# Sums of squares of keys and queries from three bfloat16 parts, on one Trainium2 core

## The chip, the core and the metric

The kernel runs on 1 core of one Trainium2 chip. Its time is the device time in microseconds (us) of one execution. Five engines take part. TensorE multiplies matrices (PE in the rows, its weight loads PEld). VectorE (DVE) and ScalarE (ACT) do elementwise work, GpSimd (POOL) a little of it, and SyncE (SP) issues most DMAs. Every engine takes its instructions in order; between engines, semaphores hold an instruction until the data it needs is there.

## What is computed

The reference is one block of a network: a pooling mixer and sparse attention, then an expert layer and a gate. The change touches only the normalization of queries and keys, for 256 tokens, 16 query heads and 4 key groups of 64 channels each:

```python
def rmsnorm(x, w):
    xf = x.astype(jnp.float32)
    y = xf * lax.rsqrt(jnp.mean(xf * xf, axis=-1, keepdims=True) + RMS_EPS)
    return (y * w.astype(jnp.float32)).astype(x.dtype)

u, q, kc, vc, ksl, vsl, kwn, vwn, gl = jnp.split(hn @ w_in[i], offsets, axis=-1)
q = rmsnorm(q.reshape(B, S, H, dk), q_norm_w[i])
k_slc = rmsnorm(ksl.reshape(B, S, G, dk), k_norm_w[i])
k_win = rmsnorm(kwn.reshape(B, S, G, dk), k_norm_w[i])
```

The mean goes over the 64 channels of one head, so for each token and head a sum of 64 squares is needed.

## The kernel before

All data is float32. A matrix of weights comes in loads of 512 KB (`load`, tile `wraw`, three buffers, issued by SP as soon as VectorE has finished with the buffer's last user). Each load is split into a high part (ScalarE, tile `whi`, L139) and the rest (VectorE, tile `wlo`, L140), and three products of the parts stand for one float32 product. `gemm` makes one tile of 128 output channels by 256 tokens in 16 steps of three products, and needs two loads; I call the first and the second load's steps the halves of a tile.

The projections run in this order: four tiles of keys and values for compression, then four tiles of keys (`head_tiles(0)`, output tile `att`), then the values (`pval`), then eight tiles of queries (`head_tiles(1)` and `head_tiles(2)`, output `qk`), then the pooling input. I number the key tiles 1 to 4 and the query tiles 1 to 8. After each of the twelve tiles, VectorE merges the result out of the accumulator (`merge`, L205), ScalarE squares it (`qsq`, L501), and a generator, `sumsq`, is put into a list of side work. The list is advanced from inside the steps of the following tile, so that TensorE's instructions for the sums come in the middle or at the end of the next tile. There `sumsq` takes the 128 channels by 256 tokens of squares as stationary weights, in two blocks of 128 tokens, against `sel2`, a matrix of 128 by 2 that picks the two heads of the tile:

```python
p = pg([128, 2, 2], "pn")
for tb in range(2):
    mm(p[:, tb], sq[:, tb * 128:tb * 128 + 128], sel2)
```

These are plain float32 products; the trace shows two passes of the array for each, four for a tile. `norm` then makes the factors of all heads when four tiles are through.

TensorE's order is the order in which the program is written (`manual_schedule` on PE). On ScalarE and VectorE a scheduler orders the instructions by its own estimates, after the prologue. In the stretch of the key tiles these two also work on the inputs of the compression: sums of the two accumulators and their scaling (`kt`, L415 to L417) and shifted copies (`kcf`, L420, ScalarE).

Of the kernel before, what the change touches and what calls it, by code (L numbers as in the profile page):

```python
# [9 lines left out]
BF = mybir.dt.bfloat16  # L10
# [3 lines left out]
OP = mybir.AluOpType  # L14
# [4 lines left out]
D, S, NH, NG, DK, NC, NE = 2048, 256, 16, 4, 64, 15, 128  # L19
# [35 lines left out]
def body(tc, I, out, dump=None):  # L55
# [4 lines left out]
    V, G, A, T = nc.vector, nc.gpsimd, nc.scalar, nc.tensor  # L60
# [9 lines left out]
    def a2(shape, name, dt=F32):  # L70
        return pools["w"].tile(shape, dt, name=name, tag="a2", bufs=7)

    def a1(shape, name, dt=F32):
        return pools["w"].tile(shape, dt, name=name, tag="a1", bufs=6)
# [4 lines left out]
    def a0(shape, name, dt=F32):  # L79
        return pools["w"].tile(shape, dt, name=name, tag="a0", bufs=12)  # L80

    def pm(shape, name="pmm"):
        return ps.tile(shape, F32, name=name, tag="mm", bufs=2)

    def pv(shape, name="pvv"):
        return ps.tile(shape, F32, name=name, tag="v", bufs=4)

    def pg(shape, name="pgg"):
        return ps.tile(shape, F32, name=name, tag="g", bufs=2)

    def mm(o, l, r, start=True, stop=True, skip=False):
        T.matmul(o, l, r, start=start, stop=stop, skip_group_check=skip)  # L92
# [22 lines left out]
    def cbv(n):  # L115
        o, w = CB[n]
        return cb[:, o:o + w]
# [32 lines left out]
    def later(g, first=False):  # L150
        gens.insert(0 if first else len(gens), [g, 0])
# [46 lines left out]
    def gemm(p, src, x, rate=0, units=None, before=None, wide=True):  # L198
        for half in range(2):
            u = units and units[half] or unit(src[:, half * 1024:(half + 1) * 1024])  # L200
            gemm_k(p, u, x, range(half * 8, half * 8 + 8), rate, before, wide)

    def merge(dst, p, rb, wide=True):
        if not wide:
            return V.tensor_tensor(dst, p[:, 0], rb, op=OP.mult)  # L205
        A.copy(dst, p[:, 1])
        V.tensor_tensor(dst, p[:, 0], dst, op=OP.add)
        return V.tensor_tensor(dst, dst, rb, op=OP.mult)
# [105 lines left out]
    def sq1(k0):  # L314
        for k in (k0, k0 + 2):
            x = xT[:, k:k + 2].rearrange("p k t -> p (k t)")
            if k == 0:
                rs["sq"] = kcf[:, 2048:2560]
                A.activation(rs["sq"], x, AF.Square)
                continue  # L320
            t = a2([128, 512], "sqb")
            A.activation(t, x, AF.Square)
            V.tensor_tensor(rs["sq"], rs["sq"], t, op=OP.add)
            if k == 14:
                V.tensor_tensor(s1.acc, rs["sq"][:, 0:256], rs["sq"][:, 256:512], op=OP.add)
# [115 lines left out]
    G.memset(kcz, 0.0)  # L441
    G.memset(vcz, 0.0)
    nc.scalar.dma_start(c1, I["cw2"])
    sel2 = cbv("sel2")
    selb = a2([128, 4, 128], "selb", F32R)
    A.copy(selb, cbv("selb").rearrange("p (c m) -> p c m", c=4))
    qw8 = a0([128, 1], "qw8")
# [1 line left out]
    def sumsq(c, sq, ms):  # L449
        yield 3  # L450
        p = pg([128, 2, 2], "pn")
        for tb in range(2):
            mm(p[:, tb], sq[:, tb * 128:tb * 128 + 128], sel2)
        V.tensor_copy(ms[:, :, 2 * c:2 * c + 2], p)
        yield

    def norm(b, ms):
        yield 2
        m2 = ms.rearrange("p t h -> p (t h)")
        V.tensor_copy(m2, rsqrt_v(m2, 16, "nr"))  # L460
        rk = a1([128, S], "rk", F32R)
        G.memset(rk.bitcast(F32), 0.0)
        yield 8
        p = pg([8, S], "pnt")
        for tb in range(2):
            T.transpose(p[:, tb * 128:tb * 128 + 128], ms[:, tb], ident)
        A.copy(rk[0:8], p)
        V.tensor_tensor(rk[32:40], p, rk.bitcast(F32)[0:8], op=OP.subtract)
        yield 4
        for c in range(4):  # L470
            p = pv([128, S], "pselb")
            mm(p, selb[:, c], rk)
            if b == 0:
                br, gp = divmod(c, 2)
                for gi in range(2):
                    h = slice(gi * 64, gi * 64 + 64)
                    V.scalar_tensor_tensor(kz[h, gp, br, gi], kraw[h, c], smv("kw")[h], p[h], op0=OP.mult, op1=OP.mult)
            else:
                q = qT[:, 4 * (b - 1) + c]
                V.scalar_tensor_tensor(q, q, qw8, p, op0=OP.mult, op1=OP.mult)  # L480
            yield
        ready.add("n%d" % b)

    def head_tiles(b, rate, ahead=None):
        ms = a0([128, 2, 8], "ms")
        for c in range(4):
            p = pm([128, 2, S])
            if b + c:
                gemm(p, I["wt"][4 * b + c], hx, rate, wide=False)
            else:  # L490
                gemm(p, I["wt"][0], hx, rate, (rs["u"], None), {1: lambda: sq1(8), 4: lambda: sq1(12), 9: rs_front}, False)
                rs["b"] = s1.rstd_back(rs["p"])
                ready.add("rstd")
            dst = kraw[:, c] if b == 0 else qT[:, 4 * (b - 1) + c]
            i = merge(dst, p, rs["b"], False)
            if b == 0 and c == 3:
                state["main"]["keys"] = i.ins
            if ahead:
                ahead(c)
            sq = a1([128, S], "qsq")  # L500
            A.activation(sq, dst, AF.Square)  # L501
            later(sumsq(c, sq, ms), True)

        def finish():
            yield 4
            yield from norm(b, ms)
        later(finish(), True)

    head_tiles(0, 0.3, load_w1)


# [71 lines left out]
    for tb in range(2):  # L583
        p = pv([128, 128], "prn")
        T.transpose(p, rs["b"][:, tb * 128:tb * 128 + 128], ident)
        V.tensor_copy(rn[:, tb:tb + 1], p[:, 0:1])
    for s, (w, kn, kl) in enumerate(((304, 3, 3), (256, 4, 4))):
        acc = [(pm, pv)[s]([128, w], "pval") for _ in range(2)]
        k0 = 0
        while k0 < KC:  # L590
# [4 lines left out]
            for k in range(n // w):  # L595
                kc = k0 + k
                a, b = hi[:, k * w:(k + 1) * w], lo[:, k * w:(k + 1) * w]
# [34 lines left out]
    def attention(gp, qb):  # L632
# [124 lines left out]
        V.tensor_tensor(t[d + (1, q)], pt, t.bitcast(F32)[d + (0, q)], op=OP.subtract)  # L757

    head_tiles(1, 0.6)
    cx = Pair("cx")  # L760
    later(attention(0, 0))
    later(attention(0, 1))
    head_tiles(2, RATE)
    later(attention(1, 0))
    later(attention(1, 1))
# [29 lines left out]
    for g in (3, 2, 1, 0):  # L795
# [4 lines left out]
        for cc in range(2):  # L800
            p = pm([128, 2, S])
# [9 lines left out]
    for m in range(KC):  # L811
        p = pm([128, 2, S])
# [302 lines left out]
    for j in range(4):  # L1115
        u = pu[0] if j == 0 else unit(I["pj"][j])
        for i in range(4):
            p = pv([128, S], "pproj")
# [26 lines left out]
    for m in range(KC):  # L1145
        gs[m] = pv([128, 2, S], "pgate")
        sq = {2 * i + 1: (lambda k=8 + 4 * m + i: s3.add(x2[:, k], pools["p"], V)) for i in range(4)} if m < 2 else None
# [113 lines left out]
```

## Time and profile before

| quantity | value |
|---|---|
| median of 3 runs | 2021.57 us (2021.44 to 2022.99) |
| the profiled execution | 2023.23 us, its span in the trace 2021.5 us |
| TensorE busy | 2011.7 us |
| VectorE, ScalarE busy | 1505.6 us, 995.6 us |
| granted TensorE clock | 1.00 of full speed, mean over the span |
| products for the sums of squares | 48 passes between 44.7 and 166.6 us |

The profile is of one execution. A timeline row gives the start of a run of equal instructions, the time from the first start to the last end, engine, source line, operation, written and read tiles, form and count; brackets at its end give the engine's idle time just before and what ended it. Neighbouring instructions of an engine overlap in such rows (the last end is modelled for TensorE), so the pace is read from start to start.

### The profile page before, as it was taken

To read this page: it belongs to the slowest core of one execution; us is meant where nothing else is said; L and a number is where in the kernel's file an instruction comes from. 1 tells how busy PE (TensorE), PEld (TensorE's weight loads), DVE (VectorE), ACT (ScalarE), POOL (GpSimd) and SP (SyncE) were. 2 spreads that over 40 slices of the span, in tenths; PEclk is the share of its full clock that TensorE was granted. 3 is DMA by queue.
4 is the path that set the end of the run, shared out by engine and by line. 5 is a ranking of instruction groups with operands and counts; after the bars stand their busy time and mean duration, and the time that the engine had idled before them with its cause. 6 is when DMAs were issued, how large, how long until landed. Compare 5 with 4: busy or idle time off the path is not lost.

```text
span 2021.5 us, 31175 instructions
## 1 busy us (share of the span) xinstructions
PE 2011.7 (100%) x11922; PEld 1733.8 (86%) x11922; DVE 1505.6 (74%) x2532; ACT 995.6 (49%) x1471; POOL 91.5 (5%) x112
## 2 busy tenths in 40 slices
PE   9999999999999999999999999999999999999999
PEld 7999988888888888888888888888888888888888
DVE  7657767767888897677777778888887555666686
ACT  6445544545444544444444454445445444455554
POOL 3100023000000000000000000000000000001000
PEclk9999999999999999999999999999999999999999
DMA  8843246655555556555555556556555666666665
GB/s 293 224 130 103 95 127 208 223 175 181 185 188 186 181 186 190 179 184 173 186 183 173 186 169 197 177 188 211 196 177 187 197 194 192 193 192 191 192 195 158
DMA packets 104469, 371.32 MB, mean 184 GB/s; under 512 B 12377, under 2 KB 14953, under 8 KB 104041
## 3 DMA queue, kind: packets, MB, share of 16 engines
q1 hardware_dynamic: 100656, 358.06, 55.6%
q10 hardware_dynamic: 1728, 6.47, 0.9%
q0 software_dynamic: 1936, 4.79, 0.9%
q8 instruction: 94, 1.54, 0.3%
q14 instruction: 55, 0.45, 0.1%
HBM read 365.05 MB, written 4.78 MB: 183 GB/s over the span
## 4 chain that ended last, share of the span: by engine, by line
PE 95%; DMA 3%; DVE 1%; ACT 1%; issue 0%; SPq 0%; ACTq 0%; DVEq 0%
PE pmm L92 45%; PE pV L92 33%; PE pgate L92 4%; PE pq L92 4%; PE pG L92 2%; DMA wraw<-in_wt_dram 1%; PE pl L92 1%; PE po L92 1%; PE pval L92 1%; PE pc L92 1%; DVE wlo L140 1%; DMA wraw<-in_w_dram 1%; PE pt L711 1%; PE pproj L92 1%; ACT whi L139 0%; DMA wraw<-in_wv_dram 0%
## 5 line engine op out<-in xcount | busy, mean ns | idle before, releaser
L140 DVE TENSOR_TENSOR wlo<-wraw,whi 128x1024 fp32r<-128x1024 f32 (+2 forms) x675 | 820.4, 1224 | 311.7 <-ACT whi L139 309.1
L139 ACT ACTIVATE whi<-wraw 128x1024 fp32r<-128x1024 f32 (+2 forms) x675 | 708.6, 1050 | 577.9 <-PE pV L92 171.7
L92 PE MATMUL pmm<-xn,whi 128*128 128x512 f32 x2048 | 716.3, 397 | 0.0
L92 PE MATMUL pV<-whi,ahl 128*128 128x512 f32 x2032 | 636.3, 391 | 0.0
L92 PE MATMUL pmm<-xn,wlo 128*128 128x256 f32 x2048 | 552.4, 280 | 0.0
L92 PEld LDWEIGHTS pV<-whi,ahl 128*128 128x128 f32 x2032 | 381.6, 188 | 78.8
L92 PEld LDWEIGHTS pmm<-xn,whi 128*128 128x128 f32 x2048 | 378.0, 188 | 79.9
L92 PE MATMUL pV<-wlo,ahl 128*128 128x512 f32 x1016 | 395.8, 390 | 0.5 <-DVE wlo L140 0.5
L92 PEld LDWEIGHTS pmm<-xn,wlo 128*128 128x128 f32 x2048 | 386.4, 189 | 9.5
L92 PEld LDWEIGHTS pV<-wlo,ahl 128*128 128x128 f32 x1016 | 190.9, 188 | 39.3 <-DVE wlo L140 1.0
L964 ACT COPY A<-pmm 128x256 f32<-128x256 f32 x112 | 41.8, 373 | 179.4 <-PE pmm L92 179.3
L1038 ACT ACTIVATE ahl<-A 128x512 fp32r<-128x512 f32 x111 | 69.8, 631 | 119.8 <-PE pV L92 118.5
L92 PE MATMUL pmm<-hn,whi 128*128 128x256 f32 x640 | 120.8, 283 | 0.0
L92 PE MATMUL pmm<-hn,wlo 128*128 128x256 f32 x320 | 106.9, 340 | 0.9 <-DVE wlo L140 0.8
L92 PEld LDWEIGHTS pmm<-hn,whi 128*128 128x128 f32 x640 | 98.5, 190 | 4.9 <-issue 3.8
L1039 DVE TENSOR_TENSOR ahl<-A,ahl 128x512 fp32r<-128x512 f32 x111 | 76.3, 690 | 34.7 <-ACT ahl L1038 33.3
L92 PE MATMUL pq<-x,whi 128*128 128x512 f32 x256 | 92.0, 400 | 0.0
L92 PE MATMUL pgate<-x,whi 128*128 128x512 f32 (+1 forms) x272 | 89.7, 385 | 0.0
L92 PE MATMUL pmm<-cx,whi 128*128 128x512 f32 x256 | 89.3, 398 | 0.0
L965 DVE TENSOR_TENSOR A<-pmm,A 128x256 f32<-128x256 f32 x112 | 47.3, 422 | 52.5 <-ACT A L964 52.2
L987 DVE TENSOR_TENSOR e<-e,gT 128x1024 f16<-128x1024 f16 x64 | 78.0, 1219 | 0.0
L981 DVE TENSOR_TENSOR oh<-idT,iob 128x1024 f16<-128x1024 bf16 x64 | 77.8, 1216 | 0.0
(284 smaller groups left out, 1907.1 us busy)
## 6 DMA issues: line engine op xcount, KB each, us to landing
wraw<-in_ut_dram SPq DMA_DIRECT2D x256, 512.0 KB, 4.2
wraw<-in_v_dram SPq DMA_DIRECT2D x256, 512.0 KB, 4.5
wraw<-in_wt_dram SPq DMA_DIRECT2D x40, 512.0 KB, 3.6
wraw<-in_wo_dram SPq DMA_DIRECT2D x32, 512.0 KB, 3.7
wraw<-in_wq_dram SPq DMA_DIRECT2D x32, 512.0 KB, 3.6
wraw<-in_wg_dram SPq DMA_DIRECT2D x32, 512.0 KB, 4.6
wraw<-in_w_dram SPq DMA_DIRECT2D x8, 512.0 KB, 4.8
wraw<-in_wv_dram SPq DMA_DIRECT2D x5, 456.0 KB, 8.4
```

The lines of the kernel that those rows point to most:

```text
L92: T.matmul(o, l, r, start=start, stop=stop, skip_group_check=skip)
L139: A.activation(hi[:, q], raw[:, q], AF.Copy)
L140: i = V.tensor_tensor(lo[:, q], raw[:, q], hi.bitcast(F32)[:, q], op=OP.subtract)
L711: T.transpose(pt[:, i, kb], e[:, i, kb * 128:kb * 128 + 128], ident)
L964: A.copy(a, p[:, 1])
L965: evac = V.tensor_tensor(a, p[:, 0], a, op=OP.add)
L981: V.tensor_tensor(oh2, idT[:, 1, t0:t0 + TB].unsqueeze(2).to_broadcast([128, TB, 128]), iob.unsqueeze(1).to_broadcast([128, TB, 128]), op= ...
L987: V.tensor_tensor(e2, e1.unsqueeze(1).to_broadcast([128, 2, TB, W]), gT[:, :, t0:t0 + TB].unsqueeze(3).to_broadcast([128, 2, TB, W]), op=O ...
L1038: A.activation(pair[:, :, 0], a, AF.Copy)
L1039: V.tensor_tensor(pair[:, :, 1], a, pair[:, :, 0].bitcast(F32), op=OP.subtract)
```

## The change

The squares are cut into three bfloat16 parts: the rounded square, the rounded rest, and what is left of that. Each part is a stationary operand of its own, `sel2` is converted to bfloat16 once, and the three products of a token block are summed in the accumulator. For a tile this puts six 16-bit products in the place of two float32 products (four passes), two conversions more on ScalarE and two subtractions more on VectorE.

```diff
-    sel2 = cbv("sel2")
+    sel2 = a0([128, 2], "sel2", BF)
+    V.tensor_copy(sel2, cbv("sel2"))
...
         for tb in range(2):
-            mm(p[:, tb], sq[:, tb * 128:tb * 128 + 128], sel2)
+            for a in range(3):
+                mm(p[:, tb], sq[:, a, tb * 128:tb * 128 + 128], sel2, start=a == 0, stop=a == 2)
...
             sq = a1([128, S], "qsq")
             A.activation(sq, dst, AF.Square)
-            later(sumsq(c, sq, ms), True)
+            sp = a2([128, 3, S], "qsp", BF)
+            A.copy(sp[:, 0], sq)
+            V.tensor_tensor(sq, sq, sp[:, 0], op=OP.subtract)
+            A.copy(sp[:, 1], sq)
+            V.tensor_tensor(sp[:, 2], sq, sp[:, 1], op=OP.subtract)
+            later(sumsq(c, sp, ms), True)
```

The four new lines are one chain: conversion (ScalarE, L505), subtraction (VectorE, L506), conversion (ScalarE, L507), subtraction (VectorE, L508). TensorE's order is the old one but for the products of the sums; in the place of each tile's four passes stand six weight loads with six products. On the other two engines the scheduler placed the chain as follows.

ScalarE at the third key tile, before (`qsq` is the tile's square; the three splits `whi` are for the values' weights):

```order
L501 ACTIVATE qsq<-att 128x256
L139 ACTIVATE whi<-wraw 128x912 x3
L501 ACTIVATE qsq<-att 128x256
```

And now:

```order
L503 ACTIVATE qsq<-att 128x256
L139 ACTIVATE whi<-wraw 128x912
L505 CAST qsp<-qsq 128x256
L139 ACTIVATE whi<-wraw 128x912
L507 CAST qsp<-qsq 128x256
L139 ACTIVATE whi<-wraw 128x912
L503 ACTIVATE qsq<-att 128x256
```

The two conversions stand between the splits of three loads of the values' weights, and the second conversion is behind the second of these splits.

VectorE at the same place, before (from the split of the third key tile's weights to the merge of the fourth, `att`):

```order
L140 TENSOR_TENSOR wlo<-wraw,whi 128x1024
L205 TENSOR_TENSOR att<-pmm,rs_456 128x256
L140 TENSOR_TENSOR wlo<-wraw,whi 128x912 x2
L205 TENSOR_TENSOR att<-pmm,rs_456 128x256
L454 COPY ms<-pn 128x2x2
```

And now:

```order
L140 TENSOR_TENSOR wlo<-wraw,whi 128x1024
L140 TENSOR_TENSOR wlo<-wraw,whi 128x912
L506 TENSOR_TENSOR qsq<-qsq,qsp 128x256
L140 TENSOR_TENSOR wlo<-wraw,whi 128x912
L508 TENSOR_TENSOR qsp<-qsq,qsp 128x256
L205 TENSOR_TENSOR att<-pmm,rs_458 128x256
```

The second subtraction, which writes the third part, is behind the split of the second load of the values' weights.

VectorE at the third and fourth query tiles, before (a merge, `qk`, and the split of weights right behind it):

```order
L205 TENSOR_TENSOR qk<-pmm,rs_456 128x256
L140 TENSOR_TENSOR wlo<-wraw,whi 128x1024
L454 COPY ms<-pn 128x2x2
L140 TENSOR_TENSOR wlo<-wraw,whi 128x1024
L205 TENSOR_TENSOR qk<-pmm,rs_456 128x256
```

And now:

```order
L205 TENSOR_TENSOR qk<-pmm,rs_458 128x256
L140 TENSOR_TENSOR wlo<-wraw,whi 128x1024
L506 TENSOR_TENSOR qsq<-qsq,qsp 128x256
L508 TENSOR_TENSOR qsp<-qsq,qsp 128x256
L456 COPY ms<-pn 128x2x2
```

The subtractions stand behind the split that follows the merge, and ahead of the copy of the sums (`ms`).

ScalarE at these tiles, before:

```order
L139 ACTIVATE whi<-wraw 128x1024 x2
L501 ACTIVATE qsq<-qk 128x256
L139 ACTIVATE whi<-wraw 128x1024 x2
L501 ACTIVATE qsq<-qk 128x256
L139 ACTIVATE whi<-wraw 128x1024 x2
```

And now:

```order
L139 ACTIVATE whi<-wraw 128x1024 x2
L503 ACTIVATE qsq<-qk 128x256
L505 CAST qsp<-qsq 128x256
L507 CAST qsp<-qsq 128x256
L139 ACTIVATE whi<-wraw 128x1024 x2
L503 ACTIVATE qsq<-qk 128x256
L505 CAST qsp<-qsq 128x256
L507 CAST qsp<-qsq 128x256
```

The conversions stand directly behind the square and ahead of the next splits.

## Rows read from the trace of the kernel before

**Rows 1.** The page, busy time of each engine, share of the span, instructions

```profile
PE 2011.7 (100%) x11922; PEld 1733.8 (86%) x11922; DVE 1505.6 (74%) x2532; ACT 995.6 (49%) x1471; POOL 91.5 (5%) x112
```

**Rows 2.** Timeline of TensorE: start us, us, engine, line, op, out<-in, form, count, [idle]

```profile
130.61 0.50 PE L92 MATMUL pn<-cb,qsq 128*128 128x2 f32 x4
130.98 0.36 PE L92 MATMUL pmm<-hn,wlo 128*128 128x256 f32 x1
```

**Rows 3.** The same, at a group of 16-bit products

```profile
828.47 0.40 PE L92 MATMUL pmm<-xn,whi 128*128 128x512 f32 x1
828.71 0.64 PE L92 MATMUL pG<-e,oh 128*128 128x64 f16 x16
829.19 0.36 PE L92 MATMUL pmm<-xn,wlo 128*128 128x256 f32 x1
```

**Rows 4.** Timeline of VectorE, query tiles: merges, one split

```profile
108.27 0.42 DVE L205 TENSOR_TENSOR qk<-pmm,rs 128x256 f32<-128x256 f32 x1 [1.57 <-PE pmm L92]
...
122.45 0.42 DVE L205 TENSOR_TENSOR qk<-pmm,rs 128x256 f32<-128x256 f32 x1 [0.62 <-PE pmm L92]
...
128.65 0.42 DVE L205 TENSOR_TENSOR qk<-pmm,rs 128x256 f32<-128x256 f32 x1 [0.51 <-PE pmm L92]
129.79 1.23 DVE L140 TENSOR_TENSOR wlo<-wraw,whi 128x1024 fp32r<-128x1024 f32 x1 [0.71 <-ACT whi L139]
...
134.97 0.42 DVE L205 TENSOR_TENSOR qk<-pmm,rs 128x256 f32<-128x256 f32 x1
...
163.11 0.42 DVE L205 TENSOR_TENSOR qk<-pmm,rs 128x256 f32<-128x256 f32 x1
```

**Rows 5.** Timeline of TensorE, the sums of squares of those query tiles

```profile
110.95 0.50 PE L92 MATMUL pn<-cb,qsq 128*128 128x2 f32 x4
...
124.77 0.50 PE L92 MATMUL pn<-cb,qsq 128*128 128x2 f32 x4
...
136.81 0.50 PE L92 MATMUL pn<-cb,qsq 128*128 128x2 f32 x4
...
166.38 0.50 PE L92 MATMUL pn<-cb,qsq 128*128 128x2 f32 x4
```

**Rows 6.** Timeline of TensorE, the key tiles

```profile
44.71 0.61 PE L92 MATMUL pn<-cb,qsq 128*128 128x2 f32 x4 [0.27 <-ACT qsq L501]
45.17 0.36 PE L92 MATMUL pmm<-hn,wlo 128*128 128x256 f32 x1
...
51.82 0.61 PE L92 MATMUL pn<-cb,qsq 128*128 128x2 f32 x4 [0.65 <-ACT qsq L501]
...
58.48 0.51 PE L92 MATMUL pn<-cb,qsq 128*128 128x2 f32 x4
...
60.35 0.41 PE L92 MATMUL pval<-whi,hn 128*128 128x304 f32 x1 [0.66 <-DVE att L205]
...
64.57 0.61 PE L92 MATMUL pn<-cb,qsq 128*128 128x2 f32 x4 [0.20 <-ACT qsq L501]
```

**Rows 7.** Timeline of ScalarE, the key tiles

```profile
43.13 1.06 ACT L139 ACTIVATE whi<-wraw 128x1024 fp32r<-128x1024 f32 x1 [2.65 <-DMA wraw<-in_wt_dram]
44.24 0.42 ACT L501 ACTIVATE qsq<-att 128x256 f32<-128x256 f32 x1
44.56 0.63 ACT L415 COPY kt<-pkv 128x256 f32<-128x256 f32 x2
...
48.03 3.30 ACT L420 COPY kcf<-kt 64x256 f32<-64x256 f32 x8
```

**Rows 8.** Timeline of VectorE, before and in the first key tiles

```profile
29.28 0.69 DVE L323 TENSOR_TENSOR kcf<-kcf,sqb 128x512 f32<-128x512 f32 x1 [1.05 <-ACT sqb L322]
...
45.36 0.75 DVE L416 TENSOR_TENSOR kt<-pkv,kt 128x256 f32<-128x256 f32 x2
```

**Rows 9.** Loads of weights issued between 44 and 62 us: time to landing

```profile
DMA to landing us min/median/max: 5.7/8.4/10.3
```

**Rows 10.** Timeline of TensorE, the warm-up products

```profile
1.23 5.91 PE L92 MATMUL idle_p<-idle_w 128*128 128x512 bf16 x18 [1.23 <-DVE idle_w L304]
```


## The prediction

> **What bounds the kernel now.** I read the page first: TensorE is busy for 2011.7 of the span's 2021.5 us, VectorE and ScalarE for three quarters and for half [rows 1]. So a microsecond that TensorE loses anywhere is a microsecond of the whole, unless it stood still nearby before and that wait goes. What the sums of squares cost on TensorE itself I read from its timeline in two places, once where nothing is waited for [rows 2], once where other 16-bit products run [rows 3]. Then I went through the timelines of VectorE, TensorE and ScalarE at the twelve tiles [rows 4 to 8], since the change makes a longer chain between a tile's merge and its sums, and asked at each tile when TensorE arrives and when the third part would be there. In the key tiles TensorE already stands still for the square: 0.27, 0.65 and 0.20 us, the brackets in [rows 6]. In the query tiles it arrives after it.
>
> **What the products cost.** The four float32 passes of a tile take from 130.61 to 130.98, 0.37 us, about 0.09 each [rows 2]. The sixteen 16-bit products with 128 by 128 weights take from 828.71 to 829.19, 0.03 each, with a weight load for every one [rows 3]. Six of them take 0.18, so a tile gains 0.19 us where nothing is waited for, 2.3 us over twelve. The new operands are narrower in the moving direction (2 columns against 64), which can only help; at the worst, at the float32 pace, six would take 0.55 and a tile would lose 0.18. I take 0.03, since these rows have the same type width and the same weights.
>
> **What the chain costs, query tiles.** Each tile now needs conversion, subtraction, conversion, subtraction between the square and the last products. Nothing in the trace converts 128 by 256 to bfloat16; the square of that shape takes 0.42 [rows 7], the copies out of the accumulator 0.63 for two [rows 7], so a conversion lies between 0.32 and 0.42, and I take 0.40. The merge, a two-operand operation of the shape, takes 0.42 [rows 4]; I take that for a subtraction. A handoff takes 0.05: the square ends at 44.24 + 0.42 = 44.66 and TensorE starts at 44.71 [rows 6, 7]. From the third part's being there to TensorE's next other work I take 0.20: with float32 it was 45.17 - 44.71 = 0.46 from the first of four passes [rows 6], plus the handoff, less four times the 0.08 by which a float32 pass in that pace is longer.
>
> VectorE's order puts the split of a load (wlo) behind the merge and ahead of the first subtraction. The split starts 129.79 - 128.65 = 1.14 after the merge, for it waits for ScalarE's part, and its 1.23 overlaps the next operation by 0.09 [rows 4]. So TensorE can go on at the merge's start + 1.14 + 1.14 + 0.42 + 0.05 + 0.40 + 0.05 + 0.42 + 0.20 = 3.82. The first conversion is hidden under that split.
>
> It went on before at the start of the sums + 0.37 [rows 2, 5]. The differences are:
> - tile 1: 108.27 + 3.82 = 112.09 against 111.32, +0.77
> - tile 3: 122.45 + 3.82 = 126.27 against 125.14, +1.13
> - tile 4: 128.65 + 3.82 = 132.47 against 130.98, +1.49
> - tile 5: 134.97 + 3.82 = 138.79 against 137.18, +1.61
> - tile 8: 163.11 + 3.82 = 166.93 against 166.75, +0.18
> - tiles 2, 6 and 7 have their merges farther ahead and gain 0.19 each: -0.57
>
> That is +4.6. The clocks of later tiles shift with TensorE, so the differences add. In tiles 5 and 6 the order puts operations of the gates and of the softmax between the two subtractions; for these I add 0.6. Query tiles: +5.2, with ends of +2.6 (conversions of 0.32, nothing added, a little less behind the chain) and +6.5.
>
> **What the chain costs, key tiles.** Here ScalarE and VectorE have other work in between, and the order counts.
> - Tile 1: the square ends at 44.66, the split of a load ends and frees VectorE at 45.36, where the `kt` sums began [rows 7, 8]. Subtraction to 45.78, conversion to 46.25, the two `kt` sums (0.75 [rows 8]) meanwhile, second subtraction 46.36 to 46.78, TensorE on at 47.0 and not at 45.17: +1.8.
> - Tile 2: its square is behind the eight `kcf` copies (3.30 [rows 7]), which can start when `kt` is scaled, at 47.1: square 50.4 to 50.8, first conversion to 51.4, subtraction to 51.9. On ScalarE a split of 1.06 [rows 7] now stands ahead of the second conversion (to 53.0), on VectorE its counterpart to 53.9 ahead of the second subtraction (54.2). TensorE goes on at 54.4; before, it went on at 51.82 + 0.46 = 52.28: +2.1 in all.
> - Tile 3: that split frees a buffer at 53.9, and the load of the second batch of values' weights is issued then. Loads took 5.7 to 10.3 us to land, 8.4 in the middle [rows 9]: 62.3. As the order stands, the second conversion is behind this load's split on ScalarE (62.35 to 63.3, a little shorter than 1.06 as it has 912 columns), the second subtraction behind its split on VectorE (63.35 to 64.4): 64.8, TensorE on at 65.0. Before: 58.48 + 0.37 = 58.85, so +6.1. It would arrive at 54.4 + 58.48 - 52.28 = 60.6, so this is a stall of about 4 us, the largest.
> - Behind it the values' second accumulator no longer waits 0.66 for the merge, which stands on VectorE behind the same chain but is done when TensorE gets there. From the sums to it TensorE needed 60.35 - 58.85 = 1.5 and now about 0.6 [rows 6]: +5.2.
> - Tile 4: TensorE arrives at 64.37 + 5.2 = 69.6. The chain is through at about 69.3 (the split of key tile 4's second half frees a buffer at 56.8, and that load lands at 65.2; VectorE then first prepares the compression's input). The old wait of 0.20 and 0.19 of passes go: +4.8.
>
> Key tiles: +4.8. With a load of 5.7 us tile 3 is over 2.6 earlier and tile 4 waits a little for its own chain: +2.0. With 10.3: +6.7. Nothing later gives this back: all that stands beside TensorE from there on is finished ahead of it.
>
> The rest of the change costs nothing. The conversion of `sel2` waits on VectorE for the constants, among the sums of `kcf`; there VectorE stood idle for 1.05 us until 29.28 [rows 8], waiting for ScalarE. If that cover were too short, its 0.2 would push one split that TensorE waits for. No DMA is added; the loads whose buffers get free later are in the key tiles' sum.
>
> **The sum.** +4.8 + 5.2 = +10.0 us. The profiled execution took 2023.23 us with a span of 2021.5, so it would be 2033.2; the median of the runs shown is 2021.57, 1.7 less, and 10.0 us on it makes 2031.6.
>
> **The rivals.**
> - The chain is hidden, and only the shorter passes count: -2.3 us, 2019.3, no change that counts. For it: ScalarE is half idle and tiles 2, 6 and 7 have the room. It decides wherever a merge is more than 3.8 us ahead of the sums' end; against it, four query tiles have 2.2 to 3.1 [rows 4, 5], and the key tiles waited for a single square [rows 6]. 0.06.
> - The key tiles cost nothing on balance: their stretch is one of loads, and if the values' loads would have held TensorE a moment later anyway, a stall ahead of them gives nothing away. Then +5.2 remains, 2026.8. For it: loads that take 8 us [rows 9]. Against it: TensorE waits for a square and a merge there and for no load [rows 6]. 0.13.
> - The stall at key tile 3 brings the slow clock back. At the start, 18 products of 512 columns took 5.91 us [rows 10], at the later pace of 828.71 - 828.47 = 0.24 [rows 3] they would take 4.3, so a second slow stretch of that kind loses 1.6: 2033.2. The Trainium skill says in TensorE: Matmul & The Clock Gate, section "HAM oscillation — how this bites in real kernels", that a matmul loop that waits for loads falls back to the low clock and starts its next work cold; this trace has a granted clock of 1.00 throughout, with no stall of that length in it. Since single products run in the middle of this stall, I give it 0.08.
>
> **How the numbers follow.** The forecast, both kinds of stalls, has 0.71; its own range is 2026 to 2035. I leave 0.02 for what I haven't thought of. A measurement of this kernel can tell about 0.2%, 4 us, from no change. The two ends of the terms added are +4.6 and +13.2, the clock's 1.6 comes on top, and the second rival starts near +2.6; so the range goes from 2025 to 2036. The first rival, and the lower part of the second, lie within 0.2%: 0.09. Faster by more than that needs a mechanism that I don't see: 0.01. Slower: 0.90.
>
> **What would show it.** In the profile after: six passes for the sums of a tile at a pace near 0.03; waits of TensorE on the sums, for `qsp` from VectorE, of 1 to 2 us at key tiles 1 and 2 and at query tiles 1, 3, 4 and 5, and over 3 us at key tile 3, ended after a load of values' weights; none at query tiles 2, 6 and 7; the stretch after 170 us unchanged in length. I am wrong if TensorE arrives at the sums after the second subtraction, if the load behind key tile 3 lands much before 60, or if the time lost up to 170 us is found again behind it.

## The result, and the profile after

| kernel | median, us | lowest to highest | mean granted clock of its executions |
|---|---|---|---|
| before | 2021.59 (4 runs) | 2021.44 to 2022.99 | 1.000 in the profiled one |
| after | 2035.50 (4 runs) | 2033.44 to 2038.53 | 1.000, 0.999, 0.996, 0.998 |

The ratio is 1.0066, with a 95% interval of 1.0054 to 1.0078: slower by 13.9 us, where +10.0 was forecast; 2035.5 lies at the upper end of the prediction's range of 2025 to 2036. The profiled execution of the changed kernel took 2033.44 us, its span is 2031.6 us, 10.1 more than that of before. Its page has TensorE no busier than before [rows 1]; the time went into standing still:

```profile
PE 2012.0 (99%) x11946; PEld 1731.9 (85%) x11946; DVE 1513.3 (74%) x2557; ACT 1002.9 (49%) x1495; POOL 91.2 (4%) x112
```

The waits of TensorE after the change (what waited and for what; us in total, times, longest):

```profile
PE pn L92 <- DVE qsp L508: 5.1, 9, 1.1
PE pn L92 <- ACT qsp L507: 4.1, 6, 1.0
PE pV L92 <- DVE wlo L140: 2.5, 3, 1.0
...
PE pn L92 <- ACT qsp L505: 0.6, 1, 0.6
PE po L92 <- ACT et L721: 0.5, 1, 0.5
```

Waits for the parts of the squares (`qsp`) make 9.8 us, where those for the square made 1.1. The other new rows, `pV` (a later product with large weights) and `po` (a product of the softmax, ahead of the sums of query tile 8), come below.

Query tile 4 shows the chain at its plainest. TensorE, the sums of its squares, which answer to [rows 2]:

```profile
133.66 0.18 PE L92 MATMUL pn<-sel,qsp 128*128 128x2 bf16 x1
134.84 0.18 PE L92 MATMUL pn<-sel,qsp 128*128 128x2 bf16 x1 [1.01 <-ACT qsp L507]
135.30 0.25 PE L92 MATMUL pn<-sel,qsp 128*128 128x2 bf16 x4 [0.28 <-DVE qsp L508]
135.42 0.37 PE L92 MATMUL pmm<-hn,wlo 128*128 128x256 f32 x1
```

ScalarE and VectorE at the same tile, which answer to the third and fourth row of [rows 4]:

```profile
132.66 0.40 ACT L503 ACTIVATE qsq<-qk 128x256 f32<-128x256 f32 x1
133.09 0.41 ACT L505 CAST qsp<-qsq 128x256 bf16<-128x256 f32 x1
134.38 0.40 ACT L507 CAST qsp<-qsq 128x256 bf16<-128x256 f32 x1 [0.88 <-DVE qsq L506]
```

```profile
131.70 0.42 DVE L205 TENSOR_TENSOR qk<-pmm,rs 128x256 f32<-128x256 f32 x1 [0.56 <-PE pmm L92]
132.79 1.23 DVE L140 TENSOR_TENSOR wlo<-wraw,whi 128x1024 fp32r<-128x1024 f32 x1 [0.67 <-ACT whi L139]
133.93 0.42 DVE L506 TENSOR_TENSOR qsq<-qsq,qsp 128x256 f32<-128x256 f32 x1
134.82 0.42 DVE L508 TENSOR_TENSOR qsp<-qsq,qsp 128x256 bf16<-128x256 f32 x1 [0.47 <-ACT qsp L507]
```

The merge starts at 131.70, the split at 132.79 (1.09 later) takes VectorE to 133.93, and then the four steps follow: subtraction at 133.93, conversion at 134.38, subtraction at 134.82, third product at 135.30. TensorE goes on at 135.42, 3.72 after the merge; 3.82 was forecast. Its first product stood at 133.66 already and waits inside the group. The last four products start from 135.30 on and the next work at 135.42, 0.03 for each.

Key tile 3, ScalarE, VectorE and TensorE, where TensorE's rows answer to the fourth of [rows 6]:

```profile
58.50 0.96 ACT L139 ACTIVATE whi<-wraw 128x912 fp32r<-128x912 f32 x1 [1.18 <-DMA wraw<-in_wv_dram]
59.37 0.39 ACT L507 CAST qsp<-qsq 128x256 bf16<-128x256 f32 x1
```

```profile
59.50 1.11 DVE L140 TENSOR_TENSOR wlo<-wraw,whi 128x912 fp32r<-128x912 f32 x1 [1.00 <-ACT whi L139]
60.52 0.42 DVE L508 TENSOR_TENSOR qsp<-qsq,qsp 128x256 bf16<-128x256 f32 x1
```

```profile
59.23 0.18 PE L92 MATMUL pn<-sel,qsp 128*128 128x2 bf16 x1
59.81 0.18 PE L92 MATMUL pn<-sel,qsp 128*128 128x2 bf16 x1 [0.40 <-ACT qsp L507]
61.00 0.25 PE L92 MATMUL pn<-sel,qsp 128*128 128x2 bf16 x4 [1.01 <-DVE qsp L508]
```

Both halves of the chain stand behind the second load's splits, as the order had it. But this load came at 58.50 and not at 62.3: it had been issued at 52.56 and landed 5.86 us later, near the shortest of [rows 9]. So the stall is 1.5 us and not 4.

How much TensorE lost at the sums of each tile, from the timeline's rows (the time from the start of the last step ahead of the sums to the start of the first behind them, after less before; the second profile is that of the repeated run below):

| tiles | forecast | first profile | second profile |
|---|---|---|---|
| query 1, 3, 4, 5 | 0.77, 1.13, 1.49, 1.61 | 0.67, 1.03, 1.39, 1.68 | the same |
| query 2, 7 | -0.19 each | -0.20, -0.20 | -0.20, -0.20 |
| query 6, 8 | -0.19 (and 0.6 for tiles 5 and 6 together), 0.18 | 0.40, -0.20 | 0.41, -0.20 |
| between the sums of query tiles 7 and 8 (`po`) | - | 0.75 | 0.75 |
| all four key tiles, from TensorE's arrival at the first | 4.8 | 2.7 | 3.9 |

### The profile page after: what moved, and what is told of

The parts are those of the page before. It is cut to its first block, busy times and chain, and to the rows that moved or that the text cites. A ratio compares the mean times of both kernels' runs of the same rounds, so it can differ in the third digit from the quotient of the medians.

```text
span 2031.6 us, 31255 instructions
## 1 busy us (share of the span) xinstructions
PE 2012.0 (99%) x11946; PEld 1731.9 (85%) x11946; DVE 1513.3 (74%) x2557; ACT 1002.9 (49%) x1495; POOL 91.2 (4%) x112
## 4 chain that ended last, share of the span: by engine, by line
PE 90%; DVE 4%; DMA 4%; ACT 2%; issue 1%; SPq 0%; ACTq 0%; DVEq 0%
PE pmm L92 44%; PE pV L92 30%; PE pgate L92 4%; PE pq L92 4%; DMA wraw<-in_v_dram 2%; DVE wlo L140 1%; PE pG L92 1%; ACT whi L139 1%; PE pl L92 1%; PE po L92 1%; PE pval L92 1%; PE pc L92 1%; DMA wraw<-in_wt_dram 1%; DMA wraw<-in_w_dram 1%; PE pt L718 1%
```

## The experiments

In all, the kernel before ran beside the changed ones on the same chip. Each median is given against the median of before in the same run, with the ratio of the two and its 95% interval.

**The products without the chain.**

```diff
-            A.activation(sq, dst, AF.Square)
-            sp = a2([128, 3, S], "qsp", BF)
...
+            sq = a2([128, 3, S], "qsp", BF)
+            A.activation(sq[:, 0], dst, AF.Square)
...
-                mm(p[:, tb], sq[:, a, tb * 128:tb * 128 + 128], sel2, start=a == 0, stop=a == 2)
+                mm(p[:, tb], sq[:, 0, tb * 128:tb * 128 + 128], sel2, start=a == 0, stop=a == 2)
```

> Leaves out the second and third part: the square is written in bfloat16 at once, and its one part goes through the array three times, so there are six 16-bit products for a tile but no chain behind the square. Theory (all of the loss is waiting for the chain): only the passes change, 0.19 us less at each of 12 tiles, 2.3 in all, 2019.3 us; six products of a tile without a wait take about 0.17 us in the trace, and TensorE waits for the sums only where it did before. Rival (the 16-bit products, with a weight load each, are what costs): the time stays well above before, 2024 us or more. If about 3 us of the loss come from something else behind 174 us (waits for loads in the product with the big values' weights), a profile of this kernel shows whether such waits come without any chain.

2027.47 us against 2022.16, ratio 1.0028 (1.0018 to 1.0038): the forecast of the theory missed by 8 us, though its price for the products holds. So without any chain the kernel is still 5 us slower than before. In its profile the query tiles gain; the key tiles lose 3.5 us from TensorE's arrival at the first sums to the end of the fourth. At each of the eight query tiles TensorE needed 0.20 us less (0.49 before, 0.29 now), and the six take 0.16 where nothing is late, as here at key tile 2. The loss stands right behind it:

```profile
50.88 0.30 PE L92 MATMUL pn<-sel,qsp 128*128 128x2 bf16 x6
51.04 0.36 PE L92 MATMUL pmm<-hn,wlo 128*128 128x256 f32 x1
...
52.83 0.50 PE L92 MATMUL pmm<-hn,whi 128*128 128x256 f32 x2 [1.20 <-ACT whi L139]
54.09 0.51 PE L92 MATMUL pmm<-hn,wlo 128*128 128x256 f32 x2 [0.76 <-DVE wlo L140]
```

ScalarE there:

```profile
44.74 3.31 ACT L420 COPY kcf<-kt 64x256 f32<-64x256 f32 x8
...
48.40 3.30 ACT L420 COPY kcf<-kt 64x256 f32<-64x256 f32 x8
51.72 2.86 ACT L139 ACTIVATE whi<-wraw 128x1024 fp32r<-128x1024 f32 x3
```

Without the conversions the scheduler put sixteen copies (`kcf`) and a square ahead of three splits of loads. TensorE stands still for 1.20 and 0.76 us. Then the clock falls (columns: stretch, us, busy time and count of TensorE, its weight loads, VectorE, ScalarE, GpSimd, granted clock, DMA share, GB/s):

```profile
50.00:54.00 4.00, 2.14 (x20) 1.69 (x18) 1.35 (x3) 3.93 (x8) 4.00 (x8) 1.00 0.79 218
...
55.00:58.00 3.00, 3.00 (x16) 3.00 (x15) 1.52 (x2) 0.00 (x0) 2.76 (x6) 0.50 0.95 216
```

TensorE had stood still for 1.9 of the 4 us to 54; the granted clock is 0.50 of full speed (1.2 GHz) from 55 to 58, though it is busy all the time there. That costs 1.7 us, and together with the stalls turns the gain into a loss; another 1.4 us are waits at `pV` (0.5 before). So a change of the chain's length in the key tiles also changes which other work the scheduler puts first, and what the key tiles lose can't be put down to waiting for the chain alone. The slow clock of the prediction's third rival (rival C below; the hidden chain is A, key tiles that cost nothing on balance are B) is no rare thing.

**The sums later.**

```diff
-        yield 3
+        yield 8
...
-            yield 4
+            yield 9
             yield from norm(b, ms)
```

> All of the change, but the sums are put into TensorE's order five steps of side work later (8 instead of 3), which is 3 us later in the query tiles and 6 us in the key tiles. Theory: the whole chain is hidden, TensorE waits for no sums, and the old waits of the key tiles (1.1 us for the square, 0.7 for the merge) go as well: 2021.6 - 2.3 - 1.8 = 2017.5 us. Rival (the two conversions and two subtractions cost by their load on ScalarE and VectorE, which make splits of weights late): the time stays near the changed kernel's, above 2028 us, with waits of TensorE for splits in place of the waits for sums.

2030.66 against 2022.16, 1.0044 (1.0031 to 1.0057). The time is in the rival's range, but not for its reason, as the next run shows. No row of a wait for `qsp` is left, and the query tiles lost nothing up to the fourth (0.20 gained at each of the four). But TensorE waited elsewhere:

```profile
PE pV L92 <- DVE wlo L140: 4.0, 4, 1.2
PE pmm L92 <- DVE wlo L140: 2.5, 1, 2.5
PE pnt L468 <- DVE ms L462: 2.4, 1, 2.4
```

What it did not lose at the sums of key tiles 1 and 2 it lost to the split of key tile 3 (2.5), and behind query tile 4 it waited for the norm's factors (2.4). Behind each the granted clock was 0.50 for some 3 us.

**The float32 sums as late.** The same two lines in the kernel before.

> The kernel before, float32 sums from the square, with the sums put five steps of side work later, as in the run that delayed the three parts. That run lost at two places though its sums waited for nothing: a wait of 2.5 us for a split at key tile 3 and one of 2.4 us for the norm's factors behind query tile 4, each with TensorE slow behind it. If the later place itself costs this (what TensorE doesn't lose at the sums it loses to the loads, and the norm comes too late), the time is 2024 to 2030 us. If the parts' work on VectorE made the norm late, it is at or below before: about 2020.

2027.26 against 2021.88, 1.0028 (1.0019 to 1.0038), in the range for the later place, with waits of 2.2 us for the split and 1.6 for the norm, and the granted clock at 0.50 behind the first: the place costs 5.4 of the 8.5 us by itself, with no bfloat16 part in it. In the profiles the parts added 0.8 to the wait for the norm, and 3.5 more were waited at `pV`, which by the runs below doesn't go with the change.

**Key tiles alone, query tiles alone.**

```diff
-            sp = a2([128, 3, S], "qsp", BF)
+            if b == 0:
+                sp = a2([128, 3, S], "qsp", BF)
...
+            else:
+                later(sumsq(c, sq, ms), True)
```

> The change in the four key tiles alone; the queries' sums stay float32 products. By the forecast's terms: +4.8 us, 2026.4. By the trace after the change (the landing of a load came at 5.9 us and not 8.4, ends of the sums against a start that was 1.4 us earlier): +2.9, 2024.5. Rival B of the prediction (given back at the loads): 2021.6. If the 3 us lost behind 174 us hang on the change in this part, they come on top.

2027.33 against 2022.16: +5.2, 1.0035 (1.0020 to 1.0050); 4.8 was forecast, the trace after the change had given 2.9, and rival B falls. Its profile has a stretch at 0.50 from 45.4 to 52.3 us, behind the sums of key tile 1, in which TensorE's products up to the sums of key tile 2 took 2.1 us longer than before. The other way round (`b > 0`):

> The change in the eight query tiles alone. By the forecast's terms: +5.2 us, 2026.8; the trace after the change gave +5.3 over the eight tiles. Rival (query tiles cost as much only because the key tiles shifted the work beside them): under 2024. If the 3 us lost behind 174 us hang on this part, 2030 or more.

2028.87: +6.7, 1.0034 (1.0021 to 1.0047). In its profile the eight tiles lose the very amounts of the table above, 5.3 with `po`, and in addition the granted clock is 0.50 from 142 to 145, behind the stalls of query tiles 3 to 5, which costs 1.5 us up to query tile 6. The two parts add up to 11.9 of the 12.8 to 13.9 of the whole.

**The chain, unread.**

```diff
-            V.tensor_tensor(sq, sq, sp[:, 0], op=OP.subtract)
-            A.copy(sp[:, 1], sq)
-            V.tensor_tensor(sp[:, 2], sq, sp[:, 1], op=OP.subtract)
-            later(sumsq(c, sp, ms), True)
+            rst = a1([128, S], "qrst")
+            V.tensor_tensor(rst, sq, sp[:, 0], op=OP.subtract)
+            A.copy(sp[:, 1], rst)
+            V.tensor_tensor(sp[:, 2], rst, sp[:, 1], op=OP.subtract)
+            later(sumsq(c, sq, ms), True)
```

> Both conversions and both subtractions are done, on a tile of their own, but nobody reads the parts: TensorE makes the float32 products from the square, as before. Theory (the query tiles' loss is waiting for the chain, not its load on ScalarE and VectorE): no waits for sums beyond those of before in the query tiles, and the time within 3 us of before, some of it in the key tiles, where the chain's operations stand between those that free the buffers of loads. Rival (the load of 24 operations more on each engine, 10 us on VectorE and 10 on ScalarE, delays splits): 2028 or more, with TensorE waiting for splits in the query tiles.

2025.78 against 2021.88: +3.9, 1.0020 (1.0011 to 1.0030), between the two. At the sums of query tiles 1 to 8 TensorE loses 0.00. It waits elsewhere:

```profile
PE pt L717 <- ACT e L708: 1.5, 1, 1.5
...
PE pselb L92 <- DVE qk L477: 0.8, 1, 0.8
...
PE po L92 <- ACT et L720: 0.5, 1, 0.5
```

The wait at `pselb` is in the norm of the keys, ahead of the query tiles. The 1.5 us at `pt` stand between the sums of query tiles 6 and 7, a wait for the softmax's exponentials; `po` comes ahead of those of tile 8. So the operations do cost by their place on ScalarE and VectorE, but not where the forecast had put them. In the changed kernel, where TensorE comes later to all this, only the wait at `po` is seen.

**The changed kernel once more, and the kernel before.** No edit.

> The changed kernel once more, beside the others on one chip. If the slow clock behind stalls belongs to it, most executions have a mean granted clock under 1.000 and lie above 2031.6 us, which the stalls alone would give, and the profile shows a stretch with a granted clock under 1 behind one of the stalls. If the waits for loads in the product with the big values' weights (2.5 us in its first profile, 0.5 before) belong to the change, they are there again; if they are chance, they differ.

2034.71 against 2021.88, 1.0071 (1.0057 to 1.0085); clocks of 0.997, 0.999, 0.997, 0.999 and 0.997. The square and TensorE at key tile 1, and stretches there and behind query tile 5:

```profile
44.77 0.42 ACT L503 ACTIVATE qsq<-att 128x256 f32<-128x256 f32 x1 [2.72 <-DVE att L205]
...
45.80 0.18 PE L92 MATMUL pn<-sel,qsp 128*128 128x2 bf16 x1 [2.70 <-ACT qsp L505]
46.77 0.18 PE L92 MATMUL pn<-sel,qsp 128*128 128x2 bf16 x1 [0.79 <-ACT qsp L507]
47.33 0.26 PE L92 MATMUL pn<-sel,qsp 128*128 128x2 bf16 x4 [0.38 <-DVE qsp L508]
```

```profile
43.00:45.00 2.00, 0.10 (x1) 0.00 (x0) 1.83 (x5) 0.23 (x1) 0.00 (x0) 1.00 0.84 320
...
47.00:49.00 2.00, 1.67 (x11) 1.68 (x12) 1.44 (x5) 1.32 (x4) 2.00 (x5) 0.50 0.82 301
...
51.00:53.00 2.00, 2.00 (x13) 2.00 (x12) 1.32 (x4) 2.00 (x5) 1.02 (x3) 0.56 0.97 224
...
146.00:148.00 2.00, 2.00 (x11) 2.00 (x11) 1.13 (x2) 0.98 (x1) 0.00 (x0) 0.50 0.00 0
```

TensorE arrived at 42.94, and its sums were through at 47.45: 4.5 us. Only a part of this is the chain: the merge of the tile started at 43.92, a microsecond after TensorE's arrival, and the square ended at 45.19. From there to 47.45 it is 2.26 us, as much as in the first profile, against 0.51 before [rows 6, 7]; so the chain adds 1.75 here, and 1.8 was forecast. While TensorE stands still the clock falls to 0.50, and it stays there until about 52.8, with TensorE busy from 47.45 on. Behind query tile 5 the same happens, in this execution and not in the first, with the same stalls ahead of it (0.67, 1.03, 1.39 and 1.68 us in some 30).

> The kernel before once more, for a second profile: how much the start (up to the first key tile, 1.4 us apart in the first two profiles) and the waits for loads in the product with the big values' weights (0.5 us in the first profile) differ between executions of one program. If they are chance: differences of 1 to 2 us at either place, and no stretch with a granted clock under 1.

2021.92, 0.9991 to 1.0011: no difference. It has no stretch under 1.00. Its first key tile comes 0.2 us earlier than in the first profile, and key tile 4 is through 1.7 us earlier, so the stretch of loads differs by over 1 us between executions of one program. Its wait for the large weights:

```profile
PE pV L92 <- DVE wlo L140: 0.4, 1, 0.4
```

0.5 and 0.4 us in the two profiles of before, 2.5 and 1.2 in the two of the changed kernel, but 0.3 and 0.2 where the change was made in the key or the query tiles alone, 1.4 without the chain, and 4.0 with late sums. In the two kernels with fillers, which have the whole change, it is 0.6 and 0.5. These waits don't go with the change in any way that I can name.

The mean granted clock by itself is no mark of the change either: of 72 executions of before in these runs, 20 have 0.999 and 52 have 1.000, and the times of the two groups don't differ. None lies lower. Of the nine executions of the changed kernel five do (0.998 to 0.996).

**Fillers.**

```diff
-        p = pg([128, 2, 2], "pn")
+        full = pg([128, 512], "pn")
+        for _ in range(fill):
+            mm(full[:, 256:512], hx[0, 0][:, 0:128], hx[0, 0])
+        p = full[:, 0:4].rearrange("p (t h) -> p t h", t=2)
...
-            later(sumsq(c, sp, ms), True)
+            later(sumsq(c, sp, ms, {0: 10, 2: 6, 4: 4, 6: 6, 7: 8, 8: 8}.get(4 * b + c, 0)), True)
```

> The changed kernel, with products that nobody reads in TensorE's order ahead of the sums, where it stood still: 10 at key tile 1, 6 at key tile 3, and 4, 6, 8 and 8 at query tiles 1, 3, 4 and 5, each 128x256 and 0.12 us long, so 0.5 to 1.2 us of a stall of 1 to 4 us is worked through. They end before the sums' third part is there and cost nothing themselves. If the slow clock comes back because TensorE stands still (rival C), the stretches at half clock become fewer: mean granted clock nearer 1.000 than in the changed kernel (0.996 to 0.999 in seven of nine executions), and about 2031 to 2033 us where the changed kernel has 2034.7. If the clock falls for another reason, nothing changes.

2032.40 against 2022.20, 1.0060 (1.0044 to 1.0076); clocks of 1.000, 1.000, 0.999, 0.999, 0.998 and, in one execution of 2042.35 us, 0.994. The longer ones (`{0: 20, 1: 8, 2: 8, 4: 6, 6: 9, 7: 12, 8: 14}`):

> The same with more of them: 20, 8 and 8 at key tiles 1 to 3, and 6, 9, 12 and 14 at query tiles 1, 3, 4 and 5 (0.7 to 2.4 us), nearly the whole of each stall. Rival C: no stretch at half clock is left, mean granted clock 1.000, and what remains is the stalls alone, 2030 to 2032 us. If fillers do not keep the clock: 2034 to 2036, and up to 1 us more where they last longer than the stall.

2033.12, 1.0060 (1.0042 to 1.0077): four executions from 2030.70 to 2033.67 with 0.999, two at 2042.7 and 2042.9 with 0.994. The profiled one is one of these:

```profile
65.00:68.00 3.00, 1.11 (x12) 0.70 (x10) 2.05 (x5) 2.16 (x5) 0.00 (x0) 1.00 0.02 7
...
69.00:93.00 24.00, 24.00 (x109) 24.00 (x108) 4.59 (x19) 4.39 (x6) 3.19 (x6) 0.51 0.49 156
```

At key tile 4, which had no filler, TensorE worked 1.11 of 3 us. Behind it the clock was at 0.50 until 93, through a stretch in which it was busy without a gap: from the sums of key tile 4 to those of query tile 1 it took 56.8 us, where before it took 45.7, so 11 us were lost. So it is not shown that fillers keep the clock: the median fell by 2.3 and 1.6 us, within the spread of the runs. What the 21 executions of the changed kernel with and without fillers do show is how time goes with the clock: 2031.3 to 2033.4 us at 1.000 (3), 2030.7 to 2034.7 at 0.999 (9), 2033.1 to 2038.5 at 0.998 to 0.996 (6), 2042.4 to 2042.9 at 0.994 (3). The profiled execution with the short fillers shows the stalls nearly alone: no stretch at 0.50, 0.6 us at `pV`, 2031.27 us, which is 9.1 more than the median of before beside it.

**Two parts.** Of the three parts the last is left out, and with it the last conversion and subtraction.

```diff
-            for a in range(3):
+            for a in range(2):
...
-            V.tensor_tensor(sq, sq, sp[:, 0], op=OP.subtract)
-            A.copy(sp[:, 1], sq)
-            V.tensor_tensor(sp[:, 2], sq, sp[:, 1], op=OP.subtract)
+            V.tensor_tensor(sp[:, 1], sq, sp[:, 0], op=OP.subtract)
```

> Two bfloat16 parts only: the last conversion and the last subtraction are left out, and with them the rest behind the second part. The chain is shorter by 0.4 + 0.05 + 0.42 + 0.05 = 0.9 us. Theory (each tile loses what the chain lacks): query tiles 3, 4 and 5 still lose 0.1, 0.4 and 0.7, the others gain 0.25, so about +0.3 over the queries and 0 to 1 in the key tiles; with what the load of the remaining operations costs (at most half of the 3.9 us of the unread chain) 2022 to 2025 us, mean clock near 1.000. Rival (the loss goes with the number of operations added, not with lateness): half of 13, 2028.

2023.95 against 2022.20, 1.0007 (0.9998 to 1.0016), as the theory had it. Query tile 4, which lost 1.39 with three parts:

```profile
131.26 0.18 PE L92 MATMUL pn<-sel,qsp 128*128 128x2 bf16 x1
132.01 0.23 PE L92 MATMUL pn<-sel,qsp 128*128 128x2 bf16 x3 [0.57 <-DVE qsp L506]
132.10 0.36 PE L92 MATMUL pmm<-hn,wlo 128*128 128x256 f32 x1
```

The second part comes with the first subtraction, and TensorE loses 0.47 (0.4 expected); tiles 3 and 5 lose 0.11 and 0.47 (0.1 and 0.7), the other five gain 0.24 or 0.25. Half of the added operations cost 1.8 us, where all of them cost 13.

**Late sums and a later norm, queries alone.** The query-only kernel with `yield 8` ahead of its sums, 9 ahead of the norm, and in `norm`:

```diff
-        yield 8
+        yield 14 if b else 8
```

> The most that the runs so far point to: the three parts in the query tiles alone, their sums five steps of side work later, and the norm's transposes six steps later still, so that TensorE waits neither for the third part nor for the norm; the key tiles as before. Theory: the eight tiles gain 0.19 each and no stall is left, no slow clock: 2022 - 1.5 = 2020.5 us. If the load of the parts on ScalarE and VectorE is what stays (3.9 us with the unread chain, at the softmax of query tiles 5 to 8): 2023 to 2026.

2023.47 against 2022.20, 1.0008 (0.9999 to 1.0016). No wait for `qsp` and none for the norm's sums (`ms`) is left, and of eleven executions eight have a clock of 1.000 and three 0.999, about the shares of the kernel before. It is the fastest of those with three parts, and like all the others no faster than the kernel before: 3.0 us above the theory's 2020.5, inside the rival's 2023 to 2026. But its waits are not all the parts' load. In its profile (2021.83 us) TensorE waits 1.0 us for `cx` (from the attention's output) and 0.2 for `rk` (from the norm); the late float32 sums have the same 1.0 and 0.2 without any part, and the kernel before has neither, so these come with the later place. Only 0.7 more (`pto`, `pt`) are not seen there.

## Why the prediction was right, and where it fell short

The sign, and the cause (TensorE arrives ahead of the third part) were right. Step by step:

- **Products: right.** 0.20 us gained in a tile where nothing is waited for; 0.19 was worked out from another line's products [rows 2, 3].
- **Query tiles: right.** Of the five tiles with a term of their own, four came within 0.1 us; tile 8 was to lose 0.18 and gained 0.20. The chain took what was reckoned (its third part was there 3.54 us after the merge), but the stop at `po`, at 171.58 us, stands between this tile's merge (169.38) and its sums (173.44), so TensorE asked for the parts 4.06 us after the merge and not 3.27 [rows 4, 5]. Tiles 5 and 6 together came 0.7 above the chain's bare terms, 0.6 had been added for what stands between the subtractions. The eight tiles' sums lose 4.6; with 0.75 for `po`, which the prediction hadn't, it is 5.3, and 5.2 was forecast. That the total fits to 0.1 is luck, the terms fit to 0.1 at four tiles.
- **Key tiles: the sum right by luck, one part wrong.** The key-only kernel lost 5.2 and 4.8 was forecast, but the 4 us of key tile 3 did not come. In the first profile the four tiles' sums cost 1.5, 0.4, 1.5 and 0.2 us, less 0.9 at the values' second accumulator; the prediction's terms were 1.8, 0.3, 4.0 and -0.4, less 0.9. So the mis-sized term is tile 3, by 2.5 us. The load landed in 5.9 us, and the prediction's +2.0 for a load of 5.7 would have been the better number (2.7 in the first profile). In three profiles with three parts in the key tiles the loss from the first key tile's arrival to the fourth's sums was 2.7, 3.9 and 5.2, the two larger ones with a stretch at 0.50, in which the products between the sums of key tiles 1 and 2 took 2.3 and 2.1 us longer (7.9 and 7.7 us, where 5.6 before). What is left of the two is 1.6 and 3.1, so the stalls alone lost less than forecast. The kernel before itself differs by 1.5 us there between its two profiles.
- **What was missing: the clock.** The prediction made rival C an alternative, of 1.6 us at one place and a chance of 0.08. It was an addition, at several places: eight of the nine executions of the changed kernel have a mean granted clock under 1.000 (the expectation above says seven), five of them 0.998 or less, which the kernel before never has, and a stretch at 0.50 cost 1.5 to 2.3 us. The Trainium skill has this in TensorE: Matmul & The Clock Gate, section "HAM oscillation — how this bites in real kernels": a loop of matmuls that waits long falls back to the low clock and starts its next work cold. The trace agrees at key tile 1 of the second profile, with 0.50 behind a wait of 4.5 us; it goes beyond that section's waits in that stalls of 0.7 to 1.7 us, one after another in the query tiles, did it too, in some executions and not in others.
- **The base.** The first profiled execution of before took 1.7 us more than the median. Counted from the second one's span of 2019.6, the changed kernel's two profiles have 12.0 and 12.9 us more, and not 10.1.
- **"Nothing later gives this back": right**, but more was lost there: 3 us behind 174 us in the first profile, nearly all at the product with the large weights. Why is open; the runs with the key tiles or the query tiles alone don't have it, and neither has the one with the short fillers, which has all of the change.

Rival A (hidden, -2.3) falls. Hiding the chain by later sums doesn't bring its gain either: where all sums came later, 8.5 us were lost to loads, to the norm and at `pV`, and where only those of the queries and their norm did, 1.3, which is within the noise. Of the 13 us, 5 are the query tiles (the chain, and `po`), which the query-only kernel, the unread chain and the two parts show each in its own way. The rest is told apart only roughly, as an estimate: some 2 to 4 in the key tiles, where chain, order and loads aren't separated, and most of the remainder the clock (a mean of 0.998 over nine executions is 4 us in 2032, a part of it while TensorE would have waited anyway).

## What to carry to other kernels

Cheaper products on the engine that bounds a kernel are worth nothing if their operands come later than that engine does: measure the time from the tile's result to the operand against the time until the engine asks for it, tile by tile, before counting passes. In a chain that alternates between two engines, the work that stands ahead of its steps in their queues counts too: at query tile 4, of 3.7 us from merge to TensorE, 2.2 passed before the first subtraction, behind a split, and 1.24 were the chain's operations. Two parts instead of three took away most of the loss. And price a stall on TensorE above its length, since the clock may fall behind it.

## What the runs showed of the hardware

- Stretches at a granted clock of 0.50 behind stalls cost 1.5 to 2.3 us, and in one profile 11, with TensorE busy throughout from 69 to 93 us. None was seen in the two profiles of the kernel before; with its float32 sums put later, and a stall of 2.2 us, it has one too.
- A stall sequence that is equal to 0.01 us in two executions brought the low clock in one and not in the other.
- A group of products whose operands come one by one starts with the first and waits inside the group; only the last operand's time sets the end (query tile 4: first product at 133.66, last four from 135.30, next work at 135.42).
